# Thirteen of 22 tile pairs of an up projection by seven products in place of eight, weights split by quarters, and chunks of 8, 8 and 6

## The chip, the cores and the metric

One core of a Trainium2 chip. The metric is the device time of one execution in microseconds (us), the median of several runs. Engines: PE (TensorE), DVE (VectorE), ACT (ScalarE), POOL (GpSimd), SP (SyncE, which here only starts transfers).

## What is computed

One step of a decoder layer in float32 for a prompt of 512 tokens and a sample group of 8 x 8 tokens, 576 tokens in all, with a model width of 1024. Cut to what matters here:

```python
h = _rmsnorm(x, norm1_w)
proj = h @ w_in                                   # (tokens, 1024) @ (1024, 3584)
ro = retention(...)                               # chunks of 128, per-head norm, swish gate
ao = dilated_attention(...)                       # three windows, keys and values of a cache too
x = x + concat([ro, ao]) @ w_out                  # (1024, 1024)
h = _rmsnorm(x, norm2_w)
ua, ub = split(h @ w_up, [D_FF])                  # D_FF = 2816, 22 tiles of 128 columns each
conv = conv_b + sum(buf[:, j:j + T] * conv_w[j] for j in range(3))   # buf: conv state, then ua
x = x + (silu(conv) * ub) @ w_down                # (2816, 1024)
y = _rmsnorm(x, normf_w)
```

Outputs are y, the retention states, the last keys and values, and the last two rows of ua, for both groups.

## The kernel before, in words

Activations stand transposed: 128 features on the partitions, 576 tokens along a row, 8 such tiles (k) for the model's width. PE multiplies in a rounded float32 format; to keep precision every operand is split into a rounded part (hi) and the rest (lo), and a product is three passes: hi x hi, hi x lo, lo x hi.

All four projections go through the helper `dense` (L245). A call makes one output tile of 128 features: for each k three passes, each as two matmuls of 288 tokens (L254), 6 per k, 48 for 8 k. Its weight tile (128 x 1024, `wraw`, three buffers) comes by a transfer on SP's queue (`w_load`, L201, asked for three to four tiles ahead), ACT makes `whi` (L219), DVE makes `wlo` (L229), two buffers each, one tile ahead.

Order: input projection with retention and attention merged between its matmuls, then the output projection (`out_proj`, L1078), then the feed-forward (`feed_forward`, L1275). The last works in two halves of 11 column tiles f. For each f, `up` (L1115) makes a dense pair: `pa` (tile f, the convolution's branch) and `pb` (tile 22+f, the gate's branch), each in a PSUM tile `d` of which there are two. `up_post` (L1124) follows: DVE scales `pa` by the norm into `ue` (L1130, L1131), ACT begins the convolution (L1134), DVE adds its other taps (L1138, L1139), ACT applies Silu (L1141), DVE scales `pb` into `g` (L1146), POOL multiplies (L1149, L1150; DVE for the last f of a half), ACT rounds (L1152, into `bhi` or `ghi`) and DVE makes the rest (L1154). After 11 pairs the down projection reads the 11 results for each of 8 output tiles, weights in pieces of 6 and 5 k; DVE adds to the residual (L1193). The last output tile (`last_down`, L1205) is done in two pieces of 320 and 256 tokens, so that the final norm of the first (`last_norm`, L1233) runs beside the second.

What stands between what is decided when the program is built: `Merge` (L96) runs the parts as coroutines, each yielding the time it expects to use on PE and the delay before its next step. Each engine then works through its own instructions in that order and waits where data or a buffer is not ready.

Of the kernel before, what the change touches and what calls it, by code (L numbers as in the profile page):

```python
# [10 lines left out]
F32 = mybir.dt.float32  # L11
# [3 lines left out]
OP = mybir.AluOpType  # L15
# [131 lines left out]
def decoder_step(ctx, tc, a):  # L147
# [33 lines left out]
    chunks = []  # L181
    IN_ORDER = [4 * sec + hp for hp in range(4) for sec in (1, 2, 0)]
    IN_ORDER += [4 * sec + hp for hp in range(4) for sec in (5, 4, 6)]
    IN_ORDER += [12 + hp for hp in range(4)]
    for m in IN_ORDER:
        chunks.append((("in", m, 0), a["w_in"], m, 0, 8))
    for m in range(8):
        chunks.append((("out", m, 0), a["w_out"], m, 0, 8))
    NFH = 11
    for half in range(2):  # L190
        for f in range(half * NFH, (half + 1) * NFH):
            chunks.append((("up", f, 0), a["w_up"], f, 0, 8))
            chunks.append((("up", NF + f, 0), a["w_up"], NF + f, 0, 8))
        for m in range(8):
            k0 = half * NFH
            chunks.append((("down", m, k0), a["w_down"], m, k0, k0 + 6))
            chunks.append((("down", m, k0 + 6), a["w_down"], m, k0 + 6, k0 + 11))
    raw, split = {}, {}
    state = {"load": 0, "use": 0}

    def w_load(upto):  # L201
        while state["load"] < min(upto, len(chunks)):
            w_load_part(state["load"], 0, 8)
            state["load"] += 1

    def w_load_part(i, c0, c1):
        _, w, m, k0, k1 = chunks[i]
        if i not in raw:
            raw[i] = wp.tile([P, 8, P], F32, name="wraw", tag="wraw", bufs=3)
        c1 = min(c1, k1 - k0)  # L210
        sp.dma_start(raw[i][:, c0:c1], wsrc(w, m, k0 + c0, k0 + c1))

    def w_split_hi(i, c0=0, c1=None):
        if i >= len(chunks) or i in split and c0 == 0:
            return
        if i not in split:
            split[i] = [wp.tile([P, 8, P], F32R, name="whi", tag="whi", bufs=2), None]
        c = slice(c0, c1 or chunks[i][4] - chunks[i][3])
        act.activation(split[i][0][:, c], raw[i][:, c], AF.Copy)  # L219

    def w_split_lo(i, c0=0, c1=None):
        if i >= len(chunks) or split[i][1] is not None and c0 == 0:
            return
        if split[i][1] is None:
            split[i][1] = wp.tile([P, 8, P], F32R, name="wlo", tag="wlo", bufs=2)
        hi, lo = split[i]
        n = chunks[i][4] - chunks[i][3]
        c = slice(c0, c1 or n)
        dve.tensor_sub(lo[:, c], raw[i][:, c], f32(hi[:, c]))  # L229
        if c.stop == n:  # L230
            raw.pop(i)

    def w_split(n):
        for i in range(state["use"], n):
            w_split_hi(i)
            w_split_lo(i)

    def w_next(key):
        i = state["use"]
        assert chunks[i][0] == key, (chunks[i][0], key)  # L240
        w_split(i + 1)
        state["use"] += 1
        return i, split.pop(i)

    def dense(ps, key, xhi, xlo, k0, k1, first, last, rows=None, made=None):  # L245

        i, (hi, lo) = w_next(key)
        w_split_hi(i + 1)
        for k in range(k0, k1):
            while made is not None and k not in made:  # L250
                yield None
            for wt, x in ((hi, xhi), (hi, xlo), (lo, xhi)):
                for s in range(2):
                    pe.matmul(ps[:, C0 + s * H2:C0 + (s + 1) * H2], wt[:, rows[k] if rows else k - k0], x[k][:, s * H2:(s + 1) * H2],  # L254
                              start=first and k == k0 and wt is hi and x is xhi,
                              stop=last and k == k1 - 1 and wt is lo)
            if k == k0 + 1:
                w_split_lo(i + 1)
            if k == k0 + 3:
                w_load(i + 4)  # L260
            yield 738.0, 0.0
# [177 lines left out]
    def in_first():  # L439
# [5 lines left out]
        for _, _, i, k in steps:  # L445
            while k not in split_k or (i, k // 4) not in wk:
                yield None
            hi, lo = split[i]
            for wt, x in ((hi, xhis), (hi, xlos), (lo, xhis)):
                for s in range(2):  # L450
                    pe.matmul(ps[i][:, C0 + s * H2:C0 + (s + 1) * H2], wt[:, k], x[k][:, s * H2:(s + 1) * H2],  # L451
                              start=k == 0 and wt is hi and x is xhis, stop=k == KD - 1 and wt is lo)
            if k == KD - 1:
                state["use"] += 1
                split.pop(i)
                if i == 0:
                    w_split_hi(2)
                    w_split_lo(2)
# [7 lines left out]
        yield from dense(first[m], ("in", m, 0), xhis, xlos, 0, KD, True, True)  # L466
# [109 lines left out]
    def in_proj():  # L576
        for m in IN_ORDER:
# [3 lines left out]
            else:  # L581
# [3 lines left out]
                for c in dense(ps, ("in", m, 0), xhis, xlos, 0, KD, True, True):  # L585
# [746 lines left out]
```

## Time and profile before

| what | value |
|---|---|
| median of 3 runs | 829.01 us (828.84 to 830.97) |
| the profiled execution | 830.02 us, of which the span on the engines is 828.2 us |
| PE busy | 809.3 us, 98% |
| DVE, ACT, POOL busy | 413.4, 294.4, 148.0 us (50%, 36%, 18%) |
| chain that ended last, PE's share | 93% |
| up and down projections | from about 388 us to the end |
| granted clock of PE | 0.997 in the mean |

The chain that ended last is followed back from the last instruction: at each step to what released it, or to the instruction before it on its engine. An engine off that chain can be late for nothing.

### The profile page before, as it was taken

What the parts mean: (1) busy time and instruction counts of PE and PEld (TensorE: products, weight loads), DVE (VectorE), ACT (ScalarE), POOL (GpSimd) and SP (SyncE); (2) the same over time, 40 slices, a digit from 0 to 9 for tenths busy, and PEclk for the clock granted to TensorE, in tenths of its full rate; (3) what the DMA queues carried; (4) which work ended last, traced back from release to release, by engine and by line L of the source; (5) the groups of instructions that cost most, each with busy time, mean ns of one, the idle gap of its engine ahead of it and who ended that gap; (6) DMA issues with size and microseconds to landing.
All of it is one profiled execution on the core that took longest, in us unless ns stands there. A gap on an engine that the chain in (4) does not pass through costs nothing.

```text
span 828.2 us, 15913 instructions
## 1 busy us (share of the span) xinstructions
PE 809.3 (98%) x6559; PEld 772.3 (93%) x6559; DVE 413.4 (50%) x792; ACT 294.4 (36%) x503; POOL 148.0 (18%) x240
## 2 busy tenths in 40 slices
PE   7999999999999999999999999999999999999995
PEld 5999999887887888999999999999999999999995
DVE  4664555665546566743545545432245545443333
ACT  5422222454535567433223323311123323332222
POOL 1321202111110213032122322100012322310111
PEclk9999999999999999999999999999999999999998
DMA  9354753678786863456255554443334455543213
GB/s 265 105 175 115 213 173 101 184 210 226 213 254 185 228 177 91 111 185 197 77 179 178 178 187 160 124 137 91 96 99 161 145 153 179 172 160 93 71 52 115
DMA packets 179798, 128.67 MB, mean 155 GB/s; under 512 B 14976, under 2 KB 176400, under 8 KB 179213
## 3 DMA queue, kind: packets, MB, share of 16 engines
q1 hardware_dynamic: 178573, 93.75, 40.4%
q10 hardware_dynamic: 928, 33.63, 11.3%
q8 instruction: 52, 0.85, 0.4%
q0 software_dynamic: 224, 0.28, 0.1%
q14 instruction: 21, 0.17, 0.1%
HBM read 121.52 MB, written 39.66 MB: 195 GB/s over the span
## 4 chain that ended last, share of the span: by engine, by line
PE 93%; ACT 3%; DVE 1%; issue 1%; DMA 1%; POOL 0%; SPq 0%; ACTq 0%; DVEq 0%
PE d L254 74%; PE m L883 2%; PE d L451 2%; PE m L928 1%; PE d L893 1%; PE m L810 1%; PE m L797 1%; PE m L496 1%; PE m L1222 1%; PE px L254 1%; PE m L666 1%; DMA wraw<-in_w_in_dram 1%; ACT s L786 1%; PE m L630 1%; PE px L410 1%
## 5 line engine op out<-in xcount | busy, mean ns | idle before, releaser
L219 ACT ACTIVATE whi<-wraw 128x1024 fp32r<-128x1024 f32 (+2 forms) x114 | 110.5, 970 | 369.2 <-issue 182.6
L229 DVE TENSOR_TENSOR wlo<-wraw,whi 128x1024 fp32r<-128x1024 f32 (+2 forms) x114 | 127.1, 1115 | 121.7 <-ACT whi L219 118.9
L254 PE MATMUL d<-bhi,whi 128*128 128x288 f32 x768 | 172.7, 306 | 1.2 <-DVE t L557 1.2
L254 PE MATMUL d<-bhi,wlo 128*128 128x288 f32 x768 | 164.2, 295 | 0.0
L254 PE MATMUL d<-blo,whi 128*128 128x288 f32 x768 | 163.9, 295 | 0.0
L254 PE MATMUL d<-hhi,whi 128*128 128x288 f32 x704 | 151.0, 296 | 0.0
L254 PE MATMUL d<-hlo,whi 128*128 128x288 f32 x704 | 150.8, 296 | 0.0
L254 PE MATMUL d<-hhi,wlo 128*128 128x288 f32 x704 | 150.7, 296 | 0.0
L254 PEld LDWEIGHTS d<-bhi,whi 128*128 128x128 f32 x768 | 121.7, 189 | 6.3 <-issue 3.1
L254 PEld LDWEIGHTS d<-bhi,wlo 128*128 128x128 f32 x768 | 123.3, 188 | 0.0
L254 PEld LDWEIGHTS d<-blo,whi 128*128 128x128 f32 x768 | 123.2, 188 | 0.0
L254 PEld LDWEIGHTS d<-hhi,whi 128*128 128x128 f32 x704 | 113.5, 189 | 0.1
L254 PEld LDWEIGHTS d<-hhi,wlo 128*128 128x128 f32 x704 | 113.5, 189 | 0.0
L254 PEld LDWEIGHTS d<-hlo,whi 128*128 128x128 f32 x704 | 113.5, 189 | 0.0
L1130 DVE TENSOR_TENSOR ue<-d,rstd_b 128x512 f32<-128x512 f32 x22 | 15.2, 691 | 74.5 <-PE d L254 74.5
L1149 POOL TENSOR_TENSOR g<-g,cv 128x512 f32<-128x512 f32 x20 | 25.8, 1289 | 142.2 <-DVE g L1146 136.7
L791 POOL TENSOR_SCALAR s<-s,sc 128x128 f32<-128x128 f32 (+3 forms) x32 | 17.3, 549 | 140.5 <-DVE sc L789 125.9
L1046 POOL TENSOR_TENSOR acc<-acc,sq 128x576 f32<-128x576 f32 x13 | 20.9, 1611 | 104.2 <-ACT sq L1045 104.2
L1135 POOL COPY cout<-ue 128x2 f32<-128x2 f32 x22 | 5.7, 260 | 137.6 <-DVE ue L1130 137.6
L884 ACT COPY kt<-m 128x384 f32<-128x384 f32 x32 | 15.3, 479 | 38.4 <-PE m L883 36.2
L883 PE MATMUL m<-ident,kc 128*128 128x128 f32 x192 | 27.4, 277 | 0.8 <-DVE sc L779 0.7
L884 DVE COPY kt<-m 128x384 f32<-128x384 f32 x32 | 17.8, 556 | 19.4 <-PE m L883 19.0
(269 smaller groups left out, 1027.3 us busy)
## 6 DMA issues: line engine op xcount, KB each, us to landing
wraw<-in_w_up_dram SPq DMA_DIRECT2D x44, 512.0 KB, 4.7
wraw<-in_w_in_dram SPq DMA_DIRECT2D x26, 512.0 KB, 3.8
kc<-in_cache_win_k_dram SPq DMA_DIRECT2D x32, 256.0 KB, 4.8
vc<-in_cache_win_v_dram SPq DMA_DIRECT2D x32, 256.0 KB, 3.2
wraw<-in_w_down_dram SPq DMA_DIRECT2D x16, 384.0 KB, 4.0
wraw<-in_w_down_dram SPq DMA_DIRECT2D x16, 320.0 KB, 3.2
kc<-in_cache_win_k_dram SPq DMA_DIRECT2D x64, 64.0 KB, 3.4
vc<-in_cache_win_v_dram SPq DMA_DIRECT2D x64, 64.0 KB, 3.3
```

Source lines behind the costliest of these rows:

```text
L219: act.activation(split[i][0][:, c], raw[i][:, c], AF.Copy)
L229: dve.tensor_sub(lo[:, c], raw[i][:, c], f32(hi[:, c]))
L254: pe.matmul(ps[:, C0 + s * H2:C0 + (s + 1) * H2], wt[:, rows[k] if rows else k - k0], x[k][:, s * H2:(s + 1) * H2], start=first and k == k ...
L410: pe.transpose(ps[:, s], xn[:r, j, k * P:(k + 1) * P], ident[:r, :r])
L451: pe.matmul(ps[i][:, C0 + s * H2:C0 + (s + 1) * H2], wt[:, k], x[k][:, s * H2:(s + 1) * H2], start=k == 0 and wt is hi and x is xhis, stop ...
L496: pe.transpose(p1[:, j * P:(j + 1) * P], src[:, j * P:(j + 1) * P], ident)
L791: pool.tensor_scalar(s[:, :n], s[:, :n], c[:, 2:3], 1.0, op0=OP.mult, op1=OP.mult)
L883: pe.transpose(ps[:, j * P:(j + 1) * P], K[u, x][:, 3 * w + j], ident)
L884: (act.copy if w else dve.tensor_copy)(kt[:, w * 384:w * 384 + 384], ps[:, :384])
L1046: pool.tensor_tensor(acc, acc, sq, op=OP.add)
L1130: dve.tensor_mul(u[:, 2:NP + 2], ya[:, :NP], rstd_b[:, :NP])
L1149: eng.tensor_tensor(g[:, :NP], g[:, :NP], c[:, :NP], op=OP.mult)
```

## The change

The up projection's pair (f, 22+f) is one product of a weight block of two by two (output tile by half of k) with an activation block of two by two (half of k by half of the tokens). For 13 of the 22 f (`SEVEN`: 2, 3, 5, 6, 8, 9, 11, 12, 14, 16, 17, 19, 20) it is made by Strassen's scheme in Winograd's form: seven products of 4 k x 3 passes x 288 tokens in place of eight. The four sums of weight quarters (`w_sum`) and the sums of the results are made on DVE, copies out of PSUM on ACT; the four sums of the activations (T1 to T4) are made once, under the output projection (`out_post`, `h_split`), whose tiles now come in the order 0, 4, 1, 5, 2, 6, 3, 7.

Weights are now split by quarters (4 k, or 3) everywhere. From the output projection on, the splits run three quarters ahead with five buffers, and raw tiles have four buffers; in the input projection both quarters of a tile are split together, as before. The gate's multiplication is on DVE for all f (`gated`). Column tiles go in chunks of 8, 8 and 6; scratch tiles share six buffers; the final norm's weights are loaded in the last chunk, into tiles that T1 to T4 leave.

The seven products accumulate in four PSUM tiles: `pa` takes the products of B11, T2 and T3 and is copied out after the first and after the second of them.

```diff
+    CHUNKS = [(0, 8), (8, 16), (16, 22)]
+    SEVEN = set(f for f in range(2, NF - 1) if f not in (4, 7, 10, 13, 15, 18))
...
+        quarters.extend([(i, slice(0, 4)), ("S1", f), (i, slice(4, 8)), ("S2", f), ("S4", f), (i + 1, slice(4, 8)),
+                         ("S3", f)])
+        reads[i], reads[i + 1] = 5, 3
+        for n, which in ((-4, "S1"), (-3, "S2"), (-2, "S4"), (-1, "S3")):
+            sums.setdefault(j + n, []).append((which, f, i))
...
+    def w_read(i):
+        reads[i] -= 1
+        if not reads[i]:
+            raw.pop(i)
+        if state["auto"]:
+            while state["load"] < len(raws) and len(raw) < (4 if state["ffn"] else 3):
+                w_load(state["load"] + 1)
...
+        if which == "S3":
+            S[which, f] = A21
+            dve.tensor_tensor(A21, A11, A21, op=OP.subtract)
...
+        if which == "S1":
+            dve.tensor_tensor(s, A21, A22, op=OP.add)
+        elif which == "S2":
+            dve.tensor_tensor(s, S["S1", f], A11, op=OP.subtract)
+        else:
+            dve.tensor_tensor(s, A12, S["S2", f], op=OP.subtract)
...
+    def ahead_of():
+        return 3 if state["ffn"] else 2
+
+    def w_begin(j):
+        for which in sums.pop(j, []):
+            w_sum(*which)
+        while state["hi"] <= min(j + ahead_of(), len(quarters) - 1):
+            if state["lo"] < state["hi"]:
+                w_lo(state["lo"])
+                state["lo"] += 1
+            w_hi(state["hi"])
+            state["hi"] += 1
...
+        t1, t2, b12 = t[:, :H2], t[:, H2:T], h1[:, H2:T]
+        dve.tensor_tensor(t1, b12, h1[:, :H2], op=OP.subtract)
+        dve.tensor_tensor(t2, h[:, H2:T], t1, op=OP.subtract)
+        yield 0.0, 700.0
+        yield from h_split("T1", k, t1)
...
+    def up_seven(f, n, ghi, glo, made):
+        j = keys["seven", f]
+        pa = dtile()[:, :H2] if f - 1 in SEVEN else mtile()[:, :H2]
+        pb, pc, pd = (mtile()[:, :H2] for _ in range(3))
+        y, z = tmp("y"), tmp("g")
+        ts = [fp.tile([P, H2], F32, name="ct", tag="ct", bufs=3) for _ in range(3)]
+        stage = []
+        order = ((pa, "B11"), (pc, "T1"), (pb, "B21"), (pa, "T2"), (pc, "B22"), (pd, "T4"), (pa, "T3"))
+        for q, (dst, c) in enumerate(order):
+            w_begin(j + q)
+            if split[j + q][1] is None:
+                w_mid(j + q)
+            hi, lo = split.pop(j + q)
+            xh, xl = TH[c]
+            for k in range(4):
+                while c[0] == "T" and (c, k) not in t_made:
+                    yield None
+                for wt, b in ((hi, xh), (hi, xl), (lo, xh)):
+                    pe.matmul(dst, wt[:, k], b[:, k], start=q in (0, 1, 2, 5) and k == 0 and wt is hi and b is xh,
+                              stop=k == 3 and wt is lo, skip_group_check=True)
+                if k == 0:
+                    w_mid(j + q)
+                yield 394.0, 0.0
+            if q == 0:
+                act.copy(ts[0], pa)
+            elif q == 1:
+                act.copy(ts[1], pc)
+            elif q == 2:
+                dve.tensor_tensor(y[:, :H2], pb, ts[0], op=OP.add)
+            elif q == 3:
+                act.copy(ts[2], pa)
+            elif q == 4:
+                dve.tensor_tensor(y[:, H2:T], pc, ts[2], op=OP.add)
+                mg.add(post_seven(f, n, pa, ts[1], y, z, stage, ghi, glo, made))
+            elif q == 5:
+                act.copy(z[:, :H2], pd)
+        stage.append(1)
...
+    def post_seven(f, n, pa, t, y, z, stage, ghi, glo, made):
...
+        dve.tensor_mul(u[:, 2:NP + 2], y[:, :NP], rstd_b[:, :NP])
...
+        act.activation(c[:, :L], u[:, 0:L], AF.Identity, scale=convw[:, 0, f:f + 1], bias=convb[:, f:f + 1])
...
+        while not stage:
+            yield None
+        yield 0.0, 300.0
+        dve.tensor_tensor(z[:, :H2], pa, z[:, :H2], op=OP.add)
+        dve.tensor_tensor(z[:, H2:T], pa, t, op=OP.add)
...
+        act.activation(c[:, :L], c[:, :L], AF.Silu)
+        dve.tensor_mul(z[:, :T], z[:, :T], rstd_b)
+        yield 0.0, 900.0
+        yield from gated(f, n, z, c, ghi, glo, made)
+
+    def gated(f, n, g, c, ghi, glo, made):
+        dve.tensor_tensor(g[:, :NP], g[:, :NP], c[:, :NP], op=OP.mult)
+        dve.tensor_tensor(by_seq(g[:, NP:T]), by_seq(g[:, NP:T]), seqs(c, 0, TS), op=OP.mult)
+        yield 0.0, 1000.0
+        act.copy(ghi[n], g[:, :T])
+        yield 0.0, 1500.0
+        dve.tensor_sub(glo[n], g[:, :T], f32(ghi[n]))
```

How it moves instructions, at three places. First DVE between two dense pairs before, one whole pair (`ue` is the scaled convolution branch, `wlo` a weight's rest, `cv` the convolution, `g` the gate's branch, `blo` the result's rest):

```order
L1130 TENSOR_TENSOR ue_4350<-d,rstd_b 128x512
L1131 TENSOR_TENSOR ue_4350<-d,rstd_b 128x8x8
L229 TENSOR_TENSOR wlo<-wraw,whi 128x1024
L1154 TENSOR_TENSOR blo<-g,bhi 128x576
L1138 SCALAR_TENSOR_TENSOR cv<-ue_4350,vec,cv 128x592
L1139 SCALAR_TENSOR_TENSOR cv<-ue_4350,vec,cv 128x592
L229 TENSOR_TENSOR wlo<-wraw,whi 128x1024
L1146 TENSOR_TENSOR g<-d,rstd_b 128x576
```

and DVE in the change from the end of pair 2 into pair 3, both by seven products (`ws` is a sum of weight quarters, `y` the convolution branch put together, `ct` a copy out of PSUM, `m` a PSUM tile):

```order
L1299 TENSOR_TENSOR ue_4469<-y,rstd_b 128x512
L1300 TENSOR_TENSOR ue_4469<-y,rstd_b 128x8x8
L270 TENSOR_TENSOR wraw<-wraw 128x512
L296 TENSOR_TENSOR wlob<-wraw,whib 128x512
L296 TENSOR_TENSOR wlo<-ws,whi 128x512
L1309 TENSOR_TENSOR g<-m,g 128x288
L1310 TENSOR_TENSOR g<-m,ct 128x288
L296 TENSOR_TENSOR wlo<-ws,whi 128x512
L1312 SCALAR_TENSOR_TENSOR cv<-ue_4469,vec,cv 128x592
L1313 SCALAR_TENSOR_TENSOR cv<-ue_4469,vec,cv 128x592
L296 TENSOR_TENSOR wlo<-wraw,whi 128x512
L1316 TENSOR_TENSOR g<-g,rstd_b 128x576
```

The instructions of a pair are shorter and about three times as many, and the first pair's second half stands between the weight quarters of the next.

Second, ACT at the same place in the change, within pair 3 (pa is `d_5527`, its copies `ct_5533` and `ct_5535`; `bhi` is the rounded result of pair 2):

```order
L1282 COPY ct_5533<-d_5527 128x288
L289 ACTIVATE whi_5555<-ws_5482 128x512
L1284 COPY ct_5534<-m_5529 128x288
L289 ACTIVATE whib_5574<-wrawb_5230 128x512
L1315 ACTIVATE cv_5503<-cv_5503 128x592
L289 ACTIVATE whi_5593<-wrawb_5230 128x512
L1325 CAST bhi_5055<-g_5380 128x576
L1288 COPY ct_5535<-d_5527 128x288
L289 ACTIVATE whi_5615<-wraw_5350 128x512
```

Before, ACT read no PSUM here; now its copies of pa stand between roundings, behind steps that wait for DVE.

Third, ACT at the last chunk's end, before

```order
L1283 ACT_TABLE_LOAD
L1283 ACTIVATE stat<-small 128x1
L219 ACTIVATE whi<-wraw 128x640
L1141 ACT_TABLE_LOAD
L1141 ACTIVATE cv<-cv 128x592
L219 ACTIVATE whi<-wraw 128x768
L1152 CAST ghi<-g 128x576
```

and in the change

```order
L1486 ACT_TABLE_LOAD
L1486 ACTIVATE stat<-small 128x1
L289 ACTIVATE whi<-wraw 128x384
L1350 ACT_TABLE_LOAD
L1350 ACTIVATE cv<-cv 128x592
L289 ACTIVATE whi<-wraw 128x384
L1325 CAST bhi<-g 128x576
```

The order is the same; the weight pieces are smaller, and behind them stand 6 k of the first down tile, where there were 11.

## Rows read from the trace of the kernel before

**Rows 1.** The page: busy us, share and count by engine; PE's granted clock by fortieths
```profile
PE 809.3 (98%) x6559; PEld 772.3 (93%) x6559; DVE 413.4 (50%) x792; ACT 294.4 (36%) x503; POOL 148.0 (18%) x240
...
PEclk9999999999999999999999999999999999999998
```

**Rows 2.** The chain that ended last, its longest piece: start us, us, engine, line
```profile
400.18 349.44 PE d L254 x2622
```

**Rows 3.** Stretches: length, then PE, PEld, DVE, ACT, POOL busy; clock; DMA share; GB/s
```profile
200.00:300.00 100.00, 97.98 (x977) 84.53 (x968) 56.68 (x150) 49.60 (x123) 11.83 (x38) 1.00 0.79 220
...
450.00:500.00 50.00, 50.00 (x377) 50.00 (x376) 23.56 (x32) 15.24 (x19) 11.56 (x20) 1.00 0.54 169
...
819.00:829.00 10.00, 0.88 (x6) 0.65 (x6) 3.00 (x10) 1.77 (x3) 0.40 (x1) 0.68 0.65 236
```

**Rows 4.** Timeline, PE in the last down tile's first piece: start us, us, instruction
```profile
813.36 0.31 PE L1222 MATMUL m<-ghi,whi 128*128 128x320 f32 x1
...
813.51 0.31 PE L1222 MATMUL m<-glo,whi 128*128 128x320 f32 x1
```

**Rows 5.** Timeline, DVE in a dense pair of the first half
```profile
447.59 0.69 DVE L1130 TENSOR_TENSOR ue<-d,rstd_b 128x512 f32<-128x512 f32 x1 [3.63 <-PE d L254]
448.20 0.22 DVE L1131 TENSOR_TENSOR ue<-d,rstd_b 128x64 f32<-128x64 f32 x1
...
449.62 0.75 DVE L1154 TENSOR_TENSOR blo<-g,bhi 128x576 fp32r<-128x576 f32 x1
450.29 0.82 DVE L1138 SCALAR_TENSOR_TENSOR cv<-ue,vec,cv 128x592 f32<-128x592 f32 x1
451.15 0.83 DVE L1139 SCALAR_TENSOR_TENSOR cv<-ue,vec,cv 128x592 f32<-128x592 f32 x1
```

**Rows 6.** Timeline of the last 12 us
```profile
817.83 1.15 ACT L1268 ACTIVATE yn<-yn,stat 128x1024 f32<-128x1024 f32 x1 [1.04 <-DVE yn L1263]
...
818.52 0.28 PE L1222 MATMUL m<-glo,whi 128*128 128x256 f32 x1
818.64 0.28 PE L1222 MATMUL m<-ghi,wlo 128*128 128x256 f32 x1
818.96 0.42 DVE L1237 TENSOR_TENSOR xT<-m,xT 128x256 f32<-128x256 f32 x1 [0.77 <-PE m L1222]
...
820.78 0.20 ACT L1255 ACTIVATE stat<-stat 128x2 f32<-128x2 f32 x1 [0.89 <-DVE stat L1252]
```

**Rows 7.** Groups by line and form: busy us, mean ns of one, idle before
```profile
L254 PEld LDWEIGHTS d<-hhi,whi 128*128 128x128 f32 x704 | 113.5, 189 | 0.1
...
L1134 ACT ACTIVATE cv<-ue,vec 128x592 f32<-128x592 f32 x22 | 19.4, 880 | 5.7 <-DVE ue L1131 5.5
...
L884 ACT COPY kt<-m 128x384 f32<-128x384 f32 x32 | 15.3, 479 | 38.4 <-PE m L883 36.2 <-PE m L943 1.1 <-POOL s L791 0.6
...
L1141 ACT ACTIVATE cv<-cv 128x592 f32<-128x592 f32 x22 | 15.0, 683 | 2.9 <-DVE cv L1139 2.9
...
L1152 ACT CAST bhi<-g 128x576 fp32r<-128x576 f32 x16 | 10.5, 657 | 0.0
...
L219 ACT ACTIVATE whi<-wraw 128x512 fp32r<-128x512 f32 x4 | 2.5, 631 | 5.8 <-DMA wraw<-in_w_in_dram 5.8
```

**Rows 8.** Waits: who for whom, us in total, times, longest
```profile
DVE wlo L229 <- ACT whi L219: 118.9, 44, 4.1
```

**Rows 9.** Timeline at the end of the second half's up projection
```profile
741.21 0.42 PE L254 MATMUL d<-hhi,wlo 128*128 128x288 f32 x2
...
742.22 1.28 ACT L1141 ACT_TABLE_LOAD   x1
...
743.51 0.70 ACT L1141 ACTIVATE cv<-cv 128x592 f32<-128x592 f32 x1
...
748.01 0.75 DVE L1154 TENSOR_TENSOR glo<-g,ghi 128x576 fp32r<-128x576 f32 x1
```

**Rows 10.** Transfers: queue, count, size, median us from issue to landing
```profile
wraw<-in_w_up_dram SPq DMA_DIRECT2D x44, 512.0 KB, 4.7
```

More of the change, by code (lines that the diff above doesn't have):

```diff
@@ L198, in decoder_step, with add_dense @@
-    raw, split = {}, {}
-    state = {"load": 0, "use": 0}
+    OUT_ORDER = [0, 4, 1, 5, 2, 6, 3, 7]
+    CHUNKS = [(0, 8), (8, 16), (16, 22)]
+    SEVEN = set(f for f in range(2, NF - 1) if f not in (4, 7, 10, 13, 15, 18))
+    reads = {}
+    def add_dense(key, w, m, k0, k1, swap=False):
+        i, n = len(raws), k1 - k0
+        raws.append((w, m, k0, k1))
+        keys[key] = len(quarters)
+        cs = (slice(0, (n + 1) // 2), slice((n + 1) // 2, n))
+        for c in cs[::-1] if swap else cs:
+            quarters.append((i, c))
+        reads[i] = 2
@@ L233, in w_split @@
[L233 to L261, printed above, removed]
+    def w_read(i):
[5 more added lines that the diff above has]
+                w_load(state["load"] + 1)
@@ new lines, in dense @@
+    def dense(ps, key, xhi, xlo, k0, k1, first, last, made=None):
+        j, k = keys[key], k0
+        while k < k1:
+            if state["ffn"]:
+                w_begin(j)
+                if split[j][1] is None:
+                    w_mid(j)
+            elif k == k0:
+                w_hi(j + 2)
+                w_hi(j + 3)
+            hi, lo = split.pop(j)
+            c = quarters[j][1]
+            for x in range(c.stop - c.start):
+                while made is not None and k not in made:
+                    yield None
+                for wt, b in ((hi, xhi), (hi, xlo), (lo, xhi)):
+                    for s in range(2):
+                        pe.matmul(ps[:, C0 + s * H2:C0 + (s + 1) * H2], wt[:, x],
+                                  b[k][:, s * H2:(s + 1) * H2],
+                                  start=first and k == k0 and wt is hi and b is xhi,
+                                  stop=last and k == k1 - 1 and wt is lo)
+                if state["ffn"]:
+                    if x == 0:
+                        w_mid(j)
+                elif k == k0 + 1:
+                    w_lo(j + 2)
+                    w_lo(j + 3)
+                    state["hi"] = state["lo"] = j + 4
+                elif k == k0 + 3:
+                    w_load(quarters[j][0] + 4)
+                k += 1
+                yield 738.0, 0.0
+            j += 1
@@ L465, in in_first @@
         first[m] = xt_tile()
-        yield from dense(first[m], ("in", m, 0), xhis, xlos, 0, KD, True, True)
+        yield from dense(first[m], ("in", m), xhis, xlos, 0, KD, True, True)
     mg.add(x_tiles())
@@ L1188, in g_tiles, with down_post @@
         t = big.tile([P, KD, T], F32R, name="b" + which, tag="b" + which, bufs=1)
-        u = fp.tile([P, NFH - KD, T], F32R, name="g" + which, tag="g" + which)
-        return [t[:, k] for k in range(KD)] + [u[:, k] for k in range(NFH - KD)]
-    def down_post(m, ps, half, yn):
+        return [t[:, k] for k in range(KD)]
+    def down_post(m, ps, last, yn):
         dve.tensor_add(xT[:, m], tok(ps), xT[:, m])
-        if half == 1:
+        if last:
             yield 0.0, 900.0
@@ L1290, in feed_forward @@
                 ps = dtile()
[L1291 to L1294 removed]
+                yield from dense(ps, ("down", m, f0), ghi, glo, 0, f1 - f0, True, True, made=made)
+                mg.add(down_post(m, ps, last, yn))
     mg.add(conv_state_in(), None)
```

303 lines of the change are left out of this document (185 added, 118 removed).

## The prediction

> **What bounds the kernel now.** I read the page first, then the chain of waits, the stretches, the groups by line and form, and last the timelines of the places that change. The page shows TensorE (PE) busy for 98% of the span at full clock, VectorE (DVE) for 50%, ScalarE (ACT) for 36% [rows 1]. A busy PE can still be a slow one, so the chain comes next: from 400 to 749 us it is one unbroken piece of matmuls of the dense helper, 2622 of them [rows 2]. Nothing waits there; the number of matmuls is the time. The stretch from 450 to 500 us has 377 in 50.00 us, **132.6 ns each** [rows 3]. So whatever takes matmuls out of the up projection shortens the kernel, as long as the other engines still keep ahead of PE. DVE and ACT feed PE: each weight tile is split into a rounded part (ACT) and the rest (DVE) before its use.
>
> The measurement tells no change from a change under 0.3%, 2.5 us.
>
> **What is removed.** A dense pair (columns f and 22+f of the up projection) takes 2 outputs x 8 k x 3 passes x 2 halves = 96 matmuls, 12.73 us. A "seven" takes 7 products x 4 k x 3 passes = 84, 11.14 us, 1.59 us a product. Thirteen pairs save 13 x 12 = 156 matmuls, 156 x 0.1326 = **20.7 us**. The tiles stay 288 wide, each matmul with its own weight load, but twelve in a row now go to the same bank. The last down tile already does that: its 320-wide matmuls start 0.15, 0.14 us apart [rows 4], and 0.145 x 288/320 = 0.130. No new price.
>
> **What is added on DVE** (lines named from here on are the changed kernel's). Durations: 512 elements 0.69, 64 elements 0.22, 576 elements 0.75, the convolution's step (592) 0.82 [rows 5], and the 288-wide sums a little over the 0.42 of a 256-wide one, 0.455 in proportion to the 0.75 of 576 [rows 6]. A seven issues 13 of 512 (7 rests of weight quarters, 4 weight sums, 1 scaling, 1 gate), 2 of 64, 4 of 288, 2 of 576, 2 of 592: 8.97 + 0.44 + 1.82 + 1.50 + 1.64 = 14.4 us, against 11.14 us of PE. A dense pair has 6 of 512 (4 rests, 1 scaling, 1 gate, which moves here from GpSimd), 2, 0, 2, 2: 7.7 us against 12.73. Two sevens and one dense pair, the pattern of the table, make 36.5 us for 35.0 us of PE: by durations DVE would be the bound. But rows follow each other faster than they last: a 512 of 0.69 is followed after 0.61, a 576 of 0.75 after 0.67, only the second convolution step, which reads the first's result, after 0.86 [rows 5]. With 0.08 less for each but the second step a seven costs 12.6, a dense pair 6.9, the group 32.1 of 35.0: 92%. I take the spacing, because that is what the next instruction sees; the durations are the upper bound.
> The Trainium skill ("VectorE: DVE Perf Modes", Terms) says that a flush follows every DVE operation and that the next cannot issue until the pipe is empty. By that the group would cost 36.5, and the change would lose part of its gain in every group; the rows here start before their predecessor ends, so the spacing stands.
>
> **Where PE will stand.** With 8% to spare, the order decides. In the second seven of a row ACT's cast of the gated result (L1325) stands ahead of the copy that empties the accumulator after its fourth product (L1288); PE needs that copy before the seventh product, 11.14 + 6 x 1.59 = 20.7 us after the first seven began. Cast (0.66) and copy (0.4, an estimate from 0.48 at 384 wide) leave 19.6 us [rows 7] for DVE to reach the end of the gate. Until there DVE has 15 x 0.61 (11 rests, 4 sums) + 3 x 0.74 (512 and 64: two gates, one scaling) + 3 x 0.67 + 5 x 0.375 + 1.60 = 16.9 us. It comes in about 1.1 us behind (the dense pair ahead hands over its own tail), and it stands for ACT. Going along both queues from the first seven's start I find: the copy after the first product (L1282) can begin at 1.8, so the rounded quarter behind it (0.53) ends at 2.7, where DVE was free at 1.7: 1.0. Twice 0.3 of the same kind. DVE's scaling ends at 11.9, ACT's first convolution step, a copy and a rounded quarter behind it at 13.6, where DVE was free at 12.5: 1.1. In all 16.9 + 1.1 + 2.7 = 20.7: **1.1 us late**. Without those stands it is in time (0); by durations it is 19.2 + 1.1 + 2.7 = 23.0, 3.4 late. That DVE does stand for ACT's weight halves is the row with 118.9 us in 44 waits, today free [rows 8]. There are four such places (2-3, 5-6, 11-12, 19-20): 4 x 1.1 = 4.4 us, bounds 0 and 14. In 8-9 and 16-17 the first seven follows a down projection: no carry, no tail of a dense pair (2.1 us), so 3.2 us earlier and no stand.
>
> **Chunk ends.** 11 and 11 become 8, 8 and 6, the matmuls of the down projection stay. Its first tile reaches the last pair's result after 7 of 8 k, 7 x 0.796 = 5.6 us, and after 5 of 6, 4.0 us, in the last chunk; before after 10 of 11, 8.0 us. At the last end the chain is long: ACT reloads a table for the Silu (742.22, 1.28 us), the Silu ends at 744.21, and the last rest begins at 748.01; the pair's last two matmuls began from 741.21 [rows 9]. From the Silu's end the bare chain is 0.61 + 0.13 + 0.66 + 0.75 and a weight quarter on each of ACT and DVE (about 0.5 each) = 3.1, so 744.2 - 741.5 + 3.1 = 5.8 us after the pair. Cover: 4.0 + 0.6 of transposes that stand there. **1.2 us late**; as long as today it would be 2.6 late, with the reload earlier 0. The two ends after 8 have no reload: 0.
>
> **The end.** The last tile's second piece covers the first piece's normalisation. It shrinks from 33 to 18 matmuls of 0.12, 1.8 us. Today the first piece's ACT step (817.83, 1.15 us) ends when PE does (818.64 + 0.28) [rows 6]; so up to 1.8 is laid bare, and the second piece's root, 2.1 us behind PE today, queues behind it. **1.1 us**, bounds 0 and 1.8.
>
> **Costed at nothing.** The input projection splits a tile as 2 x 512 in place of 1024: 2 x 0.61 where one took little less than both, hidden where DVE is busy 57% [rows 3]. Transforms of the activations, 8 subtractions of 288 and 8 splits per k pair, ride under the output projection (5.5 of 6.4 us of DVE per tile at most). Weight loads, 4.7 us to land [rows 10], are asked for four products (6.4 us) ahead at worst; if late, DVE stands in a dense pair, which has slack. SP's queue now holds the load of the final norm's weights ahead of three loads for the last down projection; it waits on a product long done.
>
> **Sum** against the profiled execution, 830.02 us: 830.0 - 20.7 + 4.4 + 1.2 + 1.1 = 816.0. The median of the runs is 1.0 below that execution, so **815.0 us**.
>
> **Rivals.**
> *Everything stays covered.* ACT's stands fall into DVE's slack: 829.0 - 20.7 + 2.3 = 810.6. For it: 92%. Against it: the order of ACT's queue. 0.20.
> *DVE is the bound*, as the durations have it: 14 us at the four places, 829.0 - 20.7 + 14 + 2.3 = 824.6. For it: two sevens and a dense pair then have no slack; against it: [rows 5]. 0.15. The flush of the Trainium skill's "VectorE: DVE Perf Modes" (Terms) would lead here.
> *Slower: the weight chain of every seven.* Sum, rounded half, rest, for a new quarter each 1.59 us, with three quarters (4.8 us) of lead. If ACT's copies, which wait for PE, and DVE's sums, which wait for loads, use up the lead in each seven, PE stands in all 13. From 18.4/13 = 1.4 us per seven the gain is gone; at 2.0 it is 829.0 - 18.4 + 26 = 836.6. For it: the waits of [rows 8], seven quarters where there were four. Against it: no stand today in 349 us, and ACT's own work per seven is 7 x 0.63 + 4 x 0.4 + 0.88 + 0.68 + 0.66 = 8.2 of 11.1 us [rows 7]. 0.09.
> *The clock falls.* Short stands at products let PE drop to 1.2 GHz; one product at that level after each of four stands costs 4 x 1.6 = 6.4, 821.4. The stretch with 2 us of stands per 100 kept 1.00, only the last 10 us, with 0.88 us of work, fell to 0.68 [rows 3]. The Trainium skill ("TensorE: Matmul & The Clock Gate", psum-queue depth-cycling) describes such a loss from short idles between groups; no row here shows it. 0.03.
> *The saving isn't there*: a matmul into the same bank again takes the 0.189 us of its weight load [rows 7]: 13 x 84 x 0.056 = 62 us more, 872. The spacing of [rows 4] speaks against it. 0.02.
>
> **Numbers.** Forecast 0.51. The range goes from all stands gone (808.3) to the DVE bound with the longer chunk end (826): 808 to 826. Under 826.5: 0.51 + 0.20 + 0.03 + 0.12 of the DVE bound = 0.86. Same: 0.03 of it and 0.01 of the weight chain, 0.04. Slower: 0.08 + 0.02 = 0.10.
>
> **What would show it.** PE's matmuls down by 156 and 132 to 133 ns apart inside a product; stands of about 1 us ahead of the seventh product of pairs 3, 6, 12 and 20, ended by the copy L1288, and none at 9 and 17; one of about 1 us in the last chunk's first down tile; DVE over 85% busy between 400 and 750 us. Stands ended by a weight half (L289, L296) in most sevens would make it wrong, and so would a DVE whose rows no longer overlap.

## The result and the profile after: 1% slower

The changed kernel takes 838.79 us (median of 6 runs, 837.58 to 841.52), the one before 829.96 us (6 runs); the ratio is **1.0105**, 95% interval 1.0084 to 1.0126. The forecast was 815.0, range 808 to 826. The profiled execution took 838.87 us, with a span of 837.1 (before 828.2).

First the page of the changed kernel, the rows that answer to [rows 1].

```profile
span 837.1 us, 16175 instructions
...
PE 797.4 (95%) x6403; PEld 753.3 (90%) x6403; DVE 535.2 (64%) x1131; ACT 354.0 (42%) x712; POOL 98.3 (12%) x199
...
PEclk9999999999999999999999999999999999999997
```

The saving is there: 6403 matmuls for 6559, 156 fewer. But PE, busy for 98% before, now stands: it has no instruction that it may begin. Whom it stands for is in the waits of PE from 385 to 830 us (who for whom: us in total, times, longest). In the kernel before, PE stood once in this stretch for more than half a microsecond, 1.03 us ahead of the last norm's sums.

```profile
PE d L1276 <- ACT ct L1288: 4.7, 4, 1.2
PE d L341 <- DVE ue L1340: 4.4, 2, 3.9
PE m L1276 <- ACT ct L1282: 2.9, 4, 0.8
PE d L341 <- ACT bhi L1325: 2.8, 3, 1.5
PE m L1276 <- ACT whib L289: 1.8, 2, 0.9
PE m L1401 <- ACT sq L1440: 1.0, 1, 1.0
PE m L1276 <- ACT whi L289: 0.9, 1, 0.9
PE d L341 <- DVE blo L1327: 0.8, 3, 0.3
PE m L1276 <- DVE wlob L296: 0.4, 2, 0.2
PE m L1276 <- DVE wlo L296: 0.2, 1, 0.2
```

Row 1 is the forecast one: four stands of 1.2 us, at the seventh product of pairs 3, 6, 12 and 20, for the copy L1288. Of the others only one was in the forecast, at the last chunk's end. A stand costs more than its idle time. At pair 6, for example, the matmuls ahead of and behind the stand begin 1.48 us apart (482.29 and 483.77) in place of 0.13, and the next two take 0.10 too long: 1.44 us for 1.18 of idle time. Most of the difference is counting: the profile lets idle time begin at the matmul's end, 0.29 us after its start, while the next would have started after 0.13. Counted from start to start, against 132.6 ns a matmul, the places cost:

| place | stands | us lost | forecast |
|---|---|---|---|
| entry: both tiles of pair 1, with the lower clock behind the second | 2 | 6.3 | 0 |
| seventh product of pairs 3, 6, 12, 20, for L1288 | 4 | 5.8 | 4.4 |
| fourth product of pairs 5, 11, 14, 19, for L1282 | 4 | 4.0 | 0 |
| third product of pairs 6, 12, 20, for both weight halves | 6 | 5.0 | 0 |
| chunk ends: last k of the first down tile, for both halves of the result | 6 | 1.6 + 1.2 + 2.2 | 0 + 0 + 1.2 |
| small delays around these | | 2.4 | 0 |
| end, from PE's last matmul of the down projection to the end of the span: 9.6 before, 12.0 now | | 2.4 | 1.1 |

These are 30.9 us of loss against the 20.7 saved, +10.2 where the spans differ by 8.9; the 1.3 between them stays unassigned. All but the entry and the end sum to 22.2 us.

How one of the places that weren't forecast comes about is in the timeline of pairs 3 to 5 (4 is dense): ACT and DVE from 458 us, and PE at the fourth product of pair 5 (start us, us, engine, instruction, idle time before it and for whom).

```profile
458.01 0.22 DVE L1323 TENSOR_TENSOR g<-g,cv 128x64 f32<-128x64 f32 x1
...
458.26 0.68 ACT L1325 CAST bhi<-g 128x576 fp32r<-128x576 f32 x1 [3.32 <-DVE g L1323]
...
459.62 0.61 ACT L289 ACTIVATE whi<-wraw 128x512 fp32r<-128x512 f32 x1
...
460.27 0.69 DVE L296 TENSOR_TENSOR wlo<-wraw,whi 128x512 fp32r<-128x512 f32 x1 [1.44 <-ACT whi L289]
...
460.88 0.75 DVE L1327 TENSOR_TENSOR blo<-g,bhi 128x576 fp32r<-128x576 f32 x1
...
462.41 0.83 DVE L1348 SCALAR_TENSOR_TENSOR cv<-ue,vec,cv 128x592 f32<-128x592 f32 x1
...
463.28 0.70 ACT L1350 ACTIVATE cv<-cv 128x592 f32<-128x592 f32 x1 [2.52 <-DVE cv L1348]
463.88 0.38 ACT L1282 COPY ct<-m 128x288 f32<-128x288 f32 x1
...
464.32 0.53 PE L1276 MATMUL m<-T,whi 128*128 128x288 f32 x2 [0.73 <-ACT ct L1282]
```

ACT stands 3.32 us at the cast of pair 3's result, because DVE is not through with the gate. Behind the cast in ACT's queue are the first convolution step of pair 4 and a weight quarter (459.62) for whose inputs no wait shows; DVE then stands 1.44 us for that quarter. So DVE's convolution steps of pair 4 end late, ACT stands 2.52 us at the Silu, and behind the Silu is the copy L1282 that PE wants. Two queues hold each other up; neither engine is full (from 425 to 500 us DVE is busy 80%, ACT 47%).

The entry, in the timeline of PE and DVE from 409 us:

```profile
409.77 0.42 PE L341 MATMUL d<-hhi,wlob 128*128 128x288 f32 x2
...
413.10 0.68 DVE L1339 TENSOR_TENSOR ue<-d,rstd_b 128x512 f32<-128x512 f32 x1
413.70 0.22 DVE L1340 TENSOR_TENSOR ue<-d,rstd_b 128x64 f32<-128x64 f32 x1
...
414.06 0.50 PE L341 MATMUL d<-hhi,whi 128*128 128x288 f32 x2 [3.87 <-DVE ue L1340]
```

and the stretches behind it, with the granted clock (columns of [rows 3]):

```profile
414.00:416.00 2.00, 1.94 (x12) 1.97 (x13) 1.97 (x5) 1.93 (x3) 0.32 (x3) 0.78 0.03 8
416.00:418.00 2.00, 2.00 (x10) 2.00 (x10) 1.97 (x4) 0.14 (x1) 0.00 (x0) 0.50 1.50 524
418.00:420.00 2.00, 2.00 (x15) 2.00 (x14) 1.43 (x3) 1.16 (x2) 0.00 (x0) 0.86 0.27 98
```

The second tile of pair 1 gets its place in PSUM (d) only when DVE has scaled what stood there (L1340), and that stands in DVE's queue behind the last output tile's sums and splits of activations, the convolution of pair 0 and the weight sums of pair 2. After these 3.87 us without work PE runs at 0.50, its 1.2 GHz level, for about 3 us (10 matmuls in 2 us in place of 15).

At the end, the rows of the last norm that answer to [rows 6], with the output transfers:

```profile
820.49 0.31 PE L1422 MATMUL m<-bhi,wlo 128*128 128x320 f32 x1
...
820.76 1.35 PE L1401 MATMUL m<-small,acc 128*128 128x1 f32 x10
...
823.85 0.71 PE L1401 MATMUL m<-small,sq 128*128 128x1 f32 x6
...
825.11 0.29 PE L1422 MATMUL m<-bhi,wlo 128*128 128x256 f32 x1
...
825.43 0.42 DVE L1437 TENSOR_TENSOR xT<-m,xT 128x256 f32<-128x256 f32 x1 [0.62 <-PE m L1422]
825.78 0.17 DVE L1457 RECIPROCAL stat<-stat 128x3 f32<-128x3 f32 x1
...
826.76 1.15 ACT L1468 ACTIVATE yn<-yn,stat 128x1024 f32<-128x1024 f32 x1 [0.40 <-DVE yn L1463]
...
827.94 4.02 SPq L1473 DMA_DIRECT2D out_dram<-yn  x5
```

The first piece's rows are ready 2.8 us after PE's last matmul (826.76 + 1.15 - 825.11), before 0.3 us (817.83 + 1.15 - 818.64 [rows 6]). From the first output transfer to the end of the span it is 9.2 us in both (before it began at 819.01). The same places before, the last matmul of the first piece and the sums of its squares:

```profile
813.65 0.31 PE L1222 MATMUL m<-ghi,wlo 128*128 128x320 f32 x1
...
815.60 0.71 PE L1203 MATMUL m<-small,sq 128*128 128x1 f32 x6
```

### The profile page after: what moved, and what is told of

Read it like the earlier page. It is cut to its first block, busy times and chain, and to the rows that moved or that the text cites. A ratio compares the mean times of both kernels' runs of the same rounds, so it can differ in the third digit from the quotient of the medians.

```text
span 837.1 us, 16175 instructions
## 1 busy us (share of the span) xinstructions
PE 797.4 (95%) x6403; PEld 753.3 (90%) x6403; DVE 535.2 (64%) x1131; ACT 354.0 (42%) x712; POOL 98.3 (12%) x199
## 4 chain that ended last, share of the span: by engine, by line
PE 73%; DVE 14%; ACT 6%; issue 4%; DMA 1%; POOL 0%; ACTq 0%; SPq 0%; DVEq 0%; POOLq 0%
PE d L341 47%; PE m L1276 5%; DVE wlo L296 3%; PE m L980 3%; PE d L546 2%; PE m L1025 2%; ACT whi L289 1%; PE d L1276 1%; DVE blo L1327 1%; PE m L907 1%; PE d L990 1%; PE m L894 1%; DVE g L1322 1%; PE m L593 1%; PE px L341 1%
## 5 line engine op out<-in xcount | busy, mean ns | idle before, releaser
L296 DVE TENSOR_TENSOR wlo<-wraw,whi 128x512 fp32r<-128x512 f32 (+1 forms) x144 | 99.9, 711 | 46.4 <-ACT whi L289 46.2
L289 ACT ACTIVATE whi<-wraw 128x512 fp32r<-128x512 f32 (+1 forms) x144 | 86.7, 618 | 72.4 <-PE d L341 63.8
L1276 PE MATMUL m<-T,whi 128*128 128x288 f32 x288 | 58.7, 296 | 2.9 <-ACT ct L1282 2.9
L341 PE MATMUL d<-hhi,whi 128*128 128x288 f32 x216 | 47.1, 300 | 4.4 <-DVE ue L1340 4.4
L1276 PEld LDWEIGHTS m<-T,whi 128*128 128x128 f32 x288 | 45.9, 188 | 3.9 <-ACT ct L1282 3.9
L341 PE MATMUL d<-hlo,whi 128*128 128x288 f32 x216 | 46.9, 298 | 0.0
L341 PE MATMUL d<-hhi,wlo 128*128 128x288 f32 x216 | 46.5, 296 | 0.0
L341 PEld LDWEIGHTS d<-hhi,whi 128*128 128x128 f32 x216 | 34.8, 190 | 5.6 <-issue 5.5
L341 PEld LDWEIGHTS d<-hhi,wlo 128*128 128x128 f32 x216 | 35.1, 191 | 0.0
L341 PEld LDWEIGHTS d<-hlo,whi 128*128 128x128 f32 x216 | 35.1, 191 | 0.0
L296 DVE TENSOR_TENSOR wlo<-ws,whi 128x512 fp32r<-128x512 f32 x35 | 24.0, 686 | 16.2 <-ACT whi L289 16.2
```

Of the source, the lines that this page charges most:

```text
L289: act.activation(split[j][0][:, :n], src, AF.Copy)
L296: dve.tensor_sub(split[j][1][:, :n], src, f32(split[j][0][:, :n]))
L341: pe.matmul(ps[:, C0 + s * H2:C0 + (s + 1) * H2], wt[:, x], b[k][:, s * H2:(s + 1) * H2], start=first and k == k0 and wt is hi and b is xh ...
L1276: pe.matmul(dst, wt[:, k], b[:, k], start=q in (0, 1, 2, 5) and k == 0 and wt is hi and b is xh, stop=k == 3 and wt is lo, skip_group_chec ...
```

## The experiments

Three theories of the loss. **D**: in a group of two sevens and a dense pair DVE has more work than PE gives it time for. **R**: the loss is in the rest of the change. **Q**: the order of the queues; on ACT, a step that waits for DVE stands ahead of what PE needs next. The first four kernels ran beside each other, against 830.02 us of the kernel before; all edits are against the changed kernel.

**No sevens.** `SEVEN` is empty, and the sums T1 to T4 are not made.

```diff
-    SEVEN = set(f for f in range(2, NF - 1) if f not in (4, 7, 10, 13, 15, 18))
+    SEVEN = set([])
...
```

> The changed kernel with no pair by seven products and no sums of activations: weight quarters, chunks of 8, 8 and 6, the gate on DVE and the new end remain. Theory Q (a step of ACT for the pair before, waiting for DVE, stands in ACT's queue ahead of a copy or weight half that PE waits for, and this needs the sevens): no stands inside pairs; left are the three chunk ends (at most 5.2 us in the changed kernel) and the longer end (2.4), so 831 to 837 us. Theory D (DVE has more work than PE gives time for in a group of two sevens and a dense pair): the same, 831 to 837. Theory R (the loss is in the rest of the change: quarters, chunks, gate, entry): the whole loss stays while the saving of 20.7 goes, 838.8 + 20.7 = 859.5 us.

831.85 us, ratio 1.0018 (1.0009 to 1.0028). R falls: quarters, chunks, the gate on DVE and the new end together cost 1.8 us. D and Q both had this. Without sevens PE does not stand at any chunk end; 0.55 and 1.01 us at the entry are left.

**The cast 1.5 us later.** One number.

```diff
-        yield 0.0, 1000.0
+        yield 0.0, 2500.0
         act.copy(ghi[n], g[:, :T])
         yield 0.0, 1500.0
         dve.tensor_sub(glo[n], g[:, :T], f32(ghi[n]))
```

> Only one number is changed: the cast of the gated result on ACT is put into the queue 1.5 us later (a delay of 2500 ns for 1000), so that it stands behind the copy of the accumulator; no engine has an instruction more or less. Theory Q: the four stands at the seventh product (1.44 us each with the restart, 5.8 in all) go, and those at the fourth product and at weight halves shrink as DVE's queue moves with it: 815 to 830 us. Theory D: the amount of DVE's work is the same, so the time is the same, 838.8 within 2 us, with the stands at other places. Theory R: the same, 838.8.

817.1 us, ratio 0.9853 (0.9831 to 0.9874): 21.7 us less than the changed kernel, with the same matmuls, DVE and ACT instructions, and faster than the one before. D falls. The stretch from 425 to 500 us, first of the changed kernel (columns of [rows 3]):

```profile
425.00:500.00 75.00, 70.79 (x521) 69.03 (x520) 60.27 (x110) 35.48 (x67) 5.64 (x18) 1.00 0.49 155
```

and of this one:

```profile
425.00:500.00 75.00, 75.00 (x567) 74.87 (x567) 65.45 (x118) 37.61 (x70) 6.82 (x18) 1.00 0.57 180
```

DVE is busy 87% (65.45 of 75) and PE never stands; in the changed kernel PE stood with DVE at 80%. The same place as above, pair 5, in this run:

```profile
453.82 0.89 ACT L1343 ACTIVATE cv<-ue,vec 128x592 f32<-128x592 f32 x1 [2.65 <-DVE ue L1340]
454.62 0.61 ACT L289 ACTIVATE whi<-wraw 128x512 fp32r<-128x512 f32 x1
455.13 0.66 ACT L1325 CAST bhi<-g 128x576 fp32r<-128x576 f32 x1
455.26 0.69 DVE L296 TENSOR_TENSOR wlo<-wraw,whi 128x512 fp32r<-128x512 f32 x1 [0.20 <-ACT whi L289]
...
457.61 0.70 ACT L1350 ACTIVATE cv<-cv 128x592 f32<-128x592 f32 x1 [1.28 <-DVE cv L1348]
...
458.21 0.38 ACT L1282 COPY ct<-m 128x288 f32<-128x288 f32 x1
```

The weight quarter now goes ahead of the cast, the cast no longer waits, DVE waits 0.20 us in place of 1.44, the Silu 1.28 in place of 2.52, and the copy is in time. Of the 3.32 us that ACT stood here, 2.65 remain, for DVE's scaling; it is not the standing that cost, but the quarter's place behind the longer wait and the cast itself. Between 415 and 785 us the cast's waiting for the gate falls from 44.0 us (21 times) to 16.6 (14), and DVE's for rounded quarters (L296 for L289) from 86.2 to 64.3.

**The gate's multiplication on GpSimd again.**

```diff
-        dve.tensor_tensor(g[:, :NP], g[:, :NP], c[:, :NP], op=OP.mult)
-        dve.tensor_tensor(by_seq(g[:, NP:T]), by_seq(g[:, NP:T]), seqs(c, 0, TS), op=OP.mult)
-        yield 0.0, 1000.0
+        e = dve if f == made['last'] else pool
+        e.tensor_tensor(g[:, :NP], g[:, :NP], c[:, :NP], op=OP.mult)
+        e.tensor_tensor(by_seq(g[:, NP:T]), by_seq(g[:, NP:T]), seqs(c, 0, TS), op=OP.mult)
+        yield 0.0, 2000.0 if e is pool else 1000.0
```

> The gate's multiplication is on GpSimd again, as before the change (not for the last column tile of a chunk): 0.75 us of DVE less per pair. Theory D: DVE's work per group of two sevens and a dense pair falls by 2.2 us, the four such groups by 9 us in all: about 829 us, and 838.8 - 9 is as low as it gets. Theory Q: the cast waits longer (GpSimd takes about 1.5 us), but goes later in the queue, behind the copy; DVE is ahead by 0.75 us at each stand: 818 to 832 us, and below 829 speaks against D. Theory R: 838.8.

831.44 us, ratio 1.0013 (1.0002 to 1.0025). It lies near what both D and Q had, and the edit also moves the cast by 1 us, so it tells nothing apart.

**Four sevens, where PE did not stand.**

```diff
-    SEVEN = set(f for f in range(2, NF - 1) if f not in (4, 7, 10, 13, 15, 18))
+    SEVEN = set([8, 9, 16, 17])
```

> Only four pairs by seven products, 8, 9, 16 and 17, those that showed no stand in the changed kernel: 48 matmuls, 6.4 us saved in place of 20.7. Theory Q: the stands inside pairs go; left are the entry (6.4 at most), the chunk ends (5.2) and the end (2.4): 825 to 837 us. Theory D: no group of two sevens and a dense pair that is short of DVE but 8 to 10 and 16 to 18, so as Q. Theory R: 838.8 + 14.3 = 853 us.

828.94 us, ratio 0.9992 (0.9983 to 1.0001), where both D and Q had it. The only stands left before the end are at the entry, 0.55 and 3.15 us. Against the run without sevens it gains 2.9 us where four sevens save 6.4; the entry, with sums of activations made again, takes part of the rest.

The next four ran beside each other, against 830.05 us. Q was now split: **Q1**, that one copy is behind the cast; **Q2**, everything behind the cast waits, and the delay is handed on.

**The copy L1288 on DVE.**

```diff
-                act.copy(ts[2], pa)
+                dve.tensor_copy(ts[2], pa)
```

> Only the copy of the accumulator after the fourth product moves, from ACT to DVE (13 copies of 288 columns, some 0.4 us each); the cast stays where it is in ACT's queue. Theory Q1 (narrow: what costs is that this one copy stands behind the cast): the four stands at the seventh product, 5.8 us in all, go: 833 us. Theory Q2 (wide: while the cast waits for DVE, everything behind it on ACT waits, the rounded weight quarters above all, and DVE then stands for those, so that the delay is handed on from pair to pair): the weight quarters still stand behind the cast, the stands move to other places, and the time stays within 3 us of 838.8.

837.83 us, ratio 1.0097 (1.0075 to 1.0119). Q1 falls. The stands change places (waits of PE, 385 to 830 us):

```profile
PE m L1276 <- DVE ct L1288: 5.3, 4, 1.3
...
PE d L1276 <- DVE ct L1288: 2.5, 4, 0.6
```

The forecast place shrinks from four times 1.2 to four times 0.6 us, and PE now stands 1.3 us for the same copy in four other sevens, 5, 11, 14 and 19, because DVE comes to it late: at pair 5 it works from 464.79 us to the copy at 469.43 with 0.30 us of standing.

**Only the casts of the sevens later.**

```diff
-        yield 0.0, 1000.0
+        yield 0.0, 2500.0 if f in SEVEN else 1000.0
```

> The cast of the gated result is put 1.5 us later into ACT's queue for the 13 pairs by seven products alone; the dense pairs keep their 1000 ns. Theory Q2: the casts of the sevens are those that wait in front of copies and weight quarters of the next pair; nearly all of the gain of the run with all casts late (817.1): 817 to 821 us. If the dense pairs' casts were what mattered (the stands at the fourth product come behind a dense pair): 830 to 836.

817.16 us, ratio 0.9844 (0.9823 to 0.9865): all of the gain. Moving the casts of the dense pairs adds nothing.

**The last sums of activations later.**

```diff
+        if last:
+            yield 0.0, 7000.0
         h1 = hs.pop(k)
```

> Only the sums and splits of the activations for the last output tile (k = 3 of T1 to T4) are emitted 7 us later, behind the scaling of the first dense pairs; casts as in the changed kernel. If the stand of 3.9 us ahead of pair 1's second tile comes from those sums standing ahead of the scaling on DVE, it shrinks by their 3 us, the clock keeps its level behind it (it fell to 0.50 for some 4 us), and the time is 838.8 - 3 to - 5 = 834 to 836. If DVE simply has too much to do there, the stand moves to pair 2: 838.8 within 1.

833.76 us, ratio 1.0037 (1.0016 to 1.0058): 5.0 us less than the changed kernel. The stand of 3.87 us becomes 1.00, nothing of it moves on, and the clock stays (same columns; before the edit 0.78 and 0.50):

```profile
414.00:416.00 2.00, 2.00 (x17) 2.00 (x16) 1.49 (x4) 1.30 (x3) 0.00 (x0) 1.00 0.55 157
416.00:418.00 2.00, 2.00 (x17) 2.00 (x16) 1.97 (x4) 0.71 (x2) 0.00 (x0) 1.00 1.52 564
```

**All of it.** Casts and last sums later, and the preload of the root's table (L1486) two down tiles later.

```diff
-                act.activation(stat[:, 39:40], ones[:, 0:1], AF.Sqrt)
...
             for m in range(KD):
+                if last and m == 2:
+                    act.activation(stat[:, 39:40], ones[:, 0:1], AF.Sqrt)
```

> All casts 1.5 us later, the last sums of activations 7 us later, and the table of the root preloaded two tiles later, behind the last Silu, so that ACT doesn't reload Silu's table ahead of it. Theory Q2: 817.1 less the 3 to 5 us of the entry, and nothing or up to 1 us at the last chunk's end (its stand is 0.3 us by then): 811 to 814 us.

**811.28 us**, ratio 0.9776 (0.9754 to 0.9798), the fastest of all, 18.8 us below the kernel before. All waits of PE from 385 to 830 us:

```profile
PE d L341 <- DVE ue L1342: 1.6, 2, 1.0
PE m L1403 <- ACT sq L1442: 1.0, 1, 1.0
```

Against the run without sevens (831.85), which has the same 1.6 us at the entry, the thirteen sevens now bring 20.6 us: the 20.7 of the forecast. The share of the preload alone wasn't measured.

**Sevens in rows of five**, in the kernel just shown (before: 830.47 us).

```diff
-    SEVEN = set(f for f in range(2, NF - 1) if f not in (4, 7, 10, 13, 15, 18))
+    SEVEN = set([2, 3, 4, 5, 6, 8, 9, 10, 11, 12, 14, 16, 17, 18, 19, 20])
```

> As the run with all casts late, the last sums late and the root's table late (811.3 us), with sevens in rows of five (pairs 2 to 6, 8 to 12, 16 to 20, and 14): 16 in place of 13, 36 matmuls or 4.8 us of PE less, and no dense pair in between to give DVE time back. By DVE's spacing (12.6 us per seven against 11.14 of PE) DVE falls 1.5 us behind per seven, 7.3 per row of five, less what slack the row begins with (0 to 6 us): 811.3 - 4.8 + 4 to 22 = 811 to 828 us, and inside the third to fifth pair of a row a seven takes at most 12.6 us. By the durations (14.4 us per seven) it falls 3.3 behind per seven, 16 per row: 835 us or more, and a seven in a row takes 14.4.

820.97 us, ratio 0.989 (0.987 to 0.9909), within the range by spacing; 9.7 us slower than with 13, though PE has 36 matmuls less. The timeline of PE, its longest stands in the first row, 13.16 us apart:

```profile
442.51 0.40 PE L1278 MATMUL m<-hhi,whi 128*128 128x288 f32 x1 [0.91 <-ACT whi L289]
...
455.67 0.40 PE L1278 MATMUL m<-hhi,whi 128*128 128x288 f32 x1 [0.91 <-ACT whi L289]
...
468.83 0.40 PE L1278 MATMUL m<-hhi,whi 128*128 128x288 f32 x1 [0.91 <-ACT whi L289]
```

and the stretch from 440 to 455 us (columns of [rows 3]):

```profile
440.00:455.00 15.00, 13.58 (x97) 12.63 (x95) 14.41 (x27) 8.17 (x17) 2.91 (x4) 1.00 0.65 212
```

Here DVE is the bound: a seven takes 13.16 us, and DVE is busy for 14.41 / 15 of that, **12.6 us**, with instructions whose durations sum to 14.3 (the 23 from 442.50 to 455.65 us). The 12.6 by spacing is measured; the expected period of at most 12.6 missed the 0.5 us that DVE waits in each.

**Cast or rest?** The delay of the second run moves two instructions, the cast on ACT and the rest of the result on DVE behind it. Two kernels took them apart (before: 830.63 us). First the rest alone later:

```diff
-        yield 0.0, 1500.0
+        yield 0.0, 3000.0
         dve.tensor_sub(glo[n], g[:, :T], f32(ghi[n]))
```

> The delay that was changed in the run with all casts late moves two instructions: the cast on ACT and, behind it, the rest of the result on DVE. Here only the rest on DVE is emitted 1.5 us later (3000 ns behind the cast for 1500); the cast keeps its place in ACT's queue. Theory Q2 (ACT's queue: the waiting cast holds up copies and weight quarters): the cast still waits in front of them, so most of the loss stays: 831 to 838 us. Theory V (DVE's queue: the rest, 0.67 us and waiting for the cast, stands ahead of the convolution's steps and so delays them): most of the gain comes, 817 to 824 us.

831.17 us, ratio 1.0004 (0.9994 to 1.0013). Then the cast alone:

```diff
-        yield 0.0, 1000.0
+        yield 0.0, 2500.0
         act.copy(ghi[n], g[:, :T])
-        yield 0.0, 1500.0
+        yield 0.0, 0.0
```

> The other half: the cast is put 1.5 us later into ACT's queue, and the rest on DVE keeps its place in time (2500 and 0 ns for 1000 and 1500), right behind the cast, so that DVE may now stand for the cast. Theory Q2: most of the gain of the run with all casts late (838.8 to 817.1), 817 to 824 us. Theory V: the rest is where it was, 832 to 838 us.

818.85 us, ratio 0.986 (0.9842 to 0.9877). The cast alone brings 19.9 of the 21.7 us. The rest alone brings 7.6, its time at the low end of what Q2 allowed: with it the four stands for L1282 are gone and those for L1288 are not (4.7 us in 4, as in the changed kernel). So the chain shown above has two links that can be cut, the weight quarter behind the cast, and the rest ahead of the convolution steps. The first is the heavier one: with the cast alone moved, stands of 2.2 us in all are left between the entry and the end.

## Why the prediction was wrong

1. *What bounds, and what is removed*: right. 156 matmuls fewer, and 20.6 us gained where nothing else stands. Twelve matmuls into one bank keep their spacing (567 in 75.00 us of the second run, 132.3 ns each).
2. *DVE's work*: right, 12.6 us per seven by spacing. The flush that the Trainium skill describes ("VectorE: DVE Perf Modes", Terms) would have made it 14.4, by the durations; the run with rows of five, where DVE is the bound, excludes that, so the measurement decides against the rule here. The rival *DVE is the bound* is out for the changed kernel as well: with the casts later DVE is busier (87%) and PE does not stand. One sign was read wrongly ahead: *"DVE over 85% busy between 400 and 750 us"* is 67% in the changed kernel (235.91 of 350 us) and 73% in the fastest one, since two down projections lie in that stretch; the 92% was worked out for a group of pairs alone.
3. *Where PE will stand*: the place, the mechanism and the size were right (four stands of 1.2 us, forecast 1.1, and none at pairs 9 and 17); that it stands nowhere else inside the pairs was not. **The step that failed is "Going along both queues"**: the queues were followed to one place, the seventh product of the second seven, and all other products were put at nothing without being followed. The fourth product (4.0 us) and the third (5.0) lie in the same two queues, and go with the same edit. The spare time of DVE did not help the instructions that stood behind a waiting one. The Trainium skill has the rule behind it: the queues of ScalarE and VectorE are strictly first in, first out ("PSUM — Partial Sum Buffer", Engine vs sequencer instructions); the trace agrees: the weight quarter at 459.62 us, for whose inputs no wait shows, begins only behind the cast that stood 3.32 us.
4. *"Weight loads ... if late, DVE stands in a dense pair, which has slack"* was said of late loads; of late roundings nothing was said. DVE stands for quarters behind the cast, 1.44 us in the dense pair 4, and hands the delay to the next seven. The slack of a dense pair was used up by waiting.
5. *Chunk ends*: "The two ends after 8 have no reload: 0" was wrong (1.6 and 1.2 us), and the last was 2.2 for 1.2. The sizes of the chunks are not the cause: without sevens, and with sevens whose casts are late, the stands there are gone but for 0.26 us at one of them. They were the same delay, handed on.
6. *"Transforms of the activations ... ride under the output projection"* failed at the last of its tiles, which has no projection behind it: 6.3 us with the clock. The run with these sums later gave 5.0 back.
7. *The end*: 2.4 us for 1.1. The shorter second piece was seen. Not seen: the sums of squares of the other tiles (L1401, ten matmuls, 1.35 us) now come behind the first piece's last matmul and not among its matmuls. So PE's work behind that matmul hardly shrinks (820.49 to 825.11, 4.6 us, before 813.65 to 818.64, 5.0), but the first piece's normalisation takes longer, 7.4 us from there to its ready rows, before 5.3: its own sums on PE stand behind the ten (823.85, 3.4 us behind, before 2.0), and its reciprocal on DVE behind the second piece's addition. That is read from the rows; no run undid it.
8. *Rivals*: *slower: the weight chain* gave 836.6 a chance of 0.09, near the measured time. That nearness is luck: it had a chain in all 13 sevens, from copies and sums that use up the lead in weights. Stands of 0.7 to 1.2 us came at 8 of them; weight halves ended those at three (5.0 us), and these too are gone when only the casts go later. *The clock falls* came true once, behind the entry's stand and not behind those of 1 us. The Trainium skill names a loss from short idle times between groups of matmuls ("TensorE: Matmul & The Clock Gate", psum-queue depth-cycling); no run here shows it, since from 425 to 500 us, with 4.2 us of idle time in stands of up to 1.2 us, the clock stayed at 1.00.

The 815.0 of the forecast is near what the kernel gives with its casts 1.5 us later (817.1), but by luck: the forecast's 4.4 us at the sevens are gone there, and the entry's 6.3 are in it. The rival *everything stays covered* (810.6) is near what it gives with the entry mended as well (811.28). How far the last 1.6 us at the entry and the end could be mended wasn't tried.

## What to carry to other kernels

When a change puts new consumers (copies out of PSUM, more and smaller weight pieces) into a queue that also holds steps waiting for another engine, go through that queue for one whole period and ask at every waiting step what stands behind it and who needs that; a share of busy time, even 80%, says nothing on it. If PE stands while the engines that feed it are not full, try the order first: here one delay of 1.5 us was worth more (21.7 us) than the arithmetic that the change saved (20.7). And where work is called hidden under a stage, look at the last turn of that stage, which has no successor to hide it.

## What was not expected of the hardware

Stands of PE of up to 1.82 us (the longest with the copy on DVE) left the granted clock at 1.00; one of 3.87 us, and one of 3.15 us with four sevens, were followed by some 3 us at 0.50, which adds about 1.5 us to the price of such a stand. And DVE's rows of 0.69 us that follow each other every 0.61 us are a rate that it keeps up when it is the bound: 96% busy over 15 us.
